# Values loaded at level 8, pooling sums as scans, the gate ahead of the root, heads 2 and 3 between more products, and the last tile's end in two pieces

## The chip, the cores and the metric

The kernel runs on one core of a Trainium2 chip. The core has a matrix engine (TensorE, PE in the profile), three engines for element work (VectorE or DVE, ScalarE or ACT, GpSimd or POOL) and a queue of transfers that SyncE (SP) issues in program order. The metric is the device time of one execution in microseconds (us); lower is better.

## The reference

A decoder layer is computed for 1024 tokens of width 1024, with 16 learned tokens ahead. Two mixers run in parallel on the normed input. One is a gated linear recurrence of four heads of 128, the other takes moving averages over 2, 4, 8 and 16 tokens. Each goes through its branch matrix and a sigmoid gate. The sum goes through an output matrix and a norm into the residual, and a gated feed-forward part with a short convolution follows. Cut to what matters here:

```python
def hgrn2(q, f_logit, i, g, lb, out_gain):
    f = lb + (1.0 - lb) * jax.nn.sigmoid(fl)
    k = (1.0 - lb) * jax.nn.sigmoid(-fl)
    ...   # state = exp(b_last) * state + k_dec^T v ;  o = q*exp(b) @ state + scores @ v, in chunks of 64
    o = o * lax.rsqrt(jnp.mean(o * o, axis=-1, keepdims=True) + EPS)
    o = o.reshape(bsz, L, HGRN_WIDTH) * out_gain
    return o * jax.nn.sigmoid(g)

def multiscale_pool(v, proj, scale):
    ...   # per group of 128 columns and window w in (2, 4, 8, 16):
        outs.append((hi - lo) / cnt - vg[:, :, gi])       # mean of the last w tokens, minus the token
    y = jnp.einsum('blgc,gcd->blgd', pooled, proj)

def reference(...):
        u = rmsnorm(h, mix_norm_pre[l])
        q, f_logit, i_in, g_out, v_pool, gate_a, gate_b = jnp.split(u @ w_in[l], cuts, axis=-1)
        a = hgrn2(q, f_logit, i_in, g_out, lbs[l], hgrn_out_norm[l])
        p = multiscale_pool(v_pool, pool_proj[l], pool_scale[l])
        z = sigmoid(gate_a) * (a @ w_branch_hgrn[l]) + sigmoid(gate_b) * (p @ w_branch_pool[l])
        h = h + rmsnorm(z @ w_out[l], mix_norm_post[l])
        u = rmsnorm(h, ffn_norm_pre[l])
        gt = causal_dwconv(u @ ffn_w_gate[l], ffn_conv_w[l], ffn_conv_b[l])
        y = (jax.nn.gelu(gt) * (u @ ffn_w_up[l])) @ ffn_w_down[l]
        h = h + rmsnorm(y, ffn_norm_post[l])
```

## The kernel before

Every matrix product is made of three products of split operands (hi by hi, hi by lo, lo by hi), so each weight block is loaded (`wraw`), rounded on ScalarE (`whi`) and its rest taken on VectorE (`wlo`). The large products use Strassen's scheme. In time the kernel has these stages:

1. 0–110 us: the values of the heads (`pv`), written to DRAM (`vscr`; the 16 learned tokens' in `vmscr`).
2. 110–325 us: the gates' and the heads' inputs by Strassen (`P`). Each head's f, q, k and kb (k over f) are stored in DRAM (`fscr`, `qscr`, `kscr`, `kbscr`), and so is its output gate (`gscr`).
3. 325–525 us: the heads, the pooling projections (`ppv` for the values, `ppp` for the outputs), two more output gates (`pg`) and the branch products (`pbb` for pooling, then `pba` for the heads).
4. 525–700 us: the output matrix (`pm`). To 1110 us the feed-forward's first matrices, to 1287 us its second by Strassen (`pd`), then the last half and the end of each 128-token tile.

The change is in stage 3 and in the end of stage 4. In stage 3 a head is a generator, `head_steps`: load f, q, kb and k; products within blocks of 2 (`sb`); then for each level 2, 4, ..., 64 the products of neighbouring blocks (`sl`, from `level_mm`), the decays multiplied into k and q (`grow`, VectorE) and the scores copied out (`level_out`); then k transposed (`pt`, `kt`), the chunks' state sums (`ds`, `st`), the output (`po`, `o`), and its mean square by products with ones (`ms`), the root by Ln and Exp on ScalarE, and the norm. All loads of a head go through SyncE's queue. The head's values (`vh`) are loaded behind its last level.

The string `ORDER` writes out what is issued in turn: h0 to h3 is a head's next step, `PVa1`/`PVb1` half of a pooling value product, `sp` the pooling split of a group, `G` an output gate product, `PP` a pooling projection, `sa` the split of a head's output for the branch products, `BB` and `BA` the branch products, `w0`–`w5` the rounding and storing in DRAM (`kept0h` and so on) of feed-forward weights for later. A scheduler of the framework then orders each engine's instructions by their dependences and this program order; in blocks named `manual_schedule` the written order holds. Tiles come from pools: 26 slots for tiles of a row's length, three buffers for each of `wraw`, `whi` and `wlo`, eight banks for products. A load of the heads or of a gate is issued behind the latest weight load in SyncE's queue (`tc.issue_after`).

Pooling: `post_pv` makes the sum of the last w values of group g by log2(w) passes of VectorE, each adding the sum shifted by 1, 2, 4, 8 (L817). `pool_split` sets the 15th column of the window 16 from a reduction (L827), divides, subtracts the value and splits (`plh`, `pll`).

The end: after the last shared products of stage 4 each of the four tiles in `c11` gets its last 18 half products, a subtraction (L1743), a square with its sum (L1667), the gain (L1668), the root and the addition to the residual (L1680, `finish`).

Of the kernel before, what the change touches and what calls it, by code (L numbers as in the profile page):

```python
# [12 lines left out]
ALU = mybir.AluOpType  # L13
# [39 lines left out]
ZA = 4  # L53
AHEAD = 3

ORDER = ("h0 h1 PV0 PVa1 h0 h1 PVb1 h0 h1 h0 PVa2 h1 sp0 h0 h1 PVb2 h0 h1 sp1 h0 h1 h2 PVa3 h0 h1 sp2 h0 h3 "
         "PVb3 h1 h0 h1 h0 h1 h2 Ga2 sp3 h0 h1 h2 h3 Gb2 h2 h3 sa0 PP0 PP1 h2 h3 Ga3 h2 h3 h2 Gb3 h3 h2 h3 PP2 PP3 h2 h3 sa1 h2 h3 w0 w1 "
         "BB0 w4 h2 h3 w4 BB1 h2 h3 BB2 sa2 h3 BB3 w5 BB4 sa3 w4 w5 BB5 w5 BB6 BB7 w5 BA0 w2 BA1 w3 BA2 BA4 BA3 BA5 BA6 BA7")
POOLED = ()
TRUNC = False  # L60

CH_ALL = [(0, 348), (348, 346), (694, 346)]
# [4 lines left out]
def trunk_kernel(ctx: ExitStack, tc: tile.TileContext, x, meta_tokens, mix_norm_pre,  # L67
# [29 lines left out]
    def slot(n, dtype=F32, name="s"):  # L97
        return stage["fm", "p"].tile([P, n], dtype, tag="fm", name=nm(name), padded_shape=[P, LP])
# [4 lines left out]
    def bank(name="ps"):  # L103
        return stage["ps", "p"].tile([P, 512], F32, tag="ps", name=nm(name))
# [11 lines left out]
    def small(shape, name, tag, bufs=4):  # L116
        return sm.tile(shape, F32, tag=tag, name=nm(name), bufs=bufs)
# [63 lines left out]
    def mm3(ps, a, b, first, last):  # L181
        (ahi, alo), (bhi, blo) = a, b
        pe.matmul(ps, ahi, bhi, start=first, stop=False)  # L183
        pe.matmul(ps, ahi, blo, start=False, stop=False)  # L184
        pe.matmul(ps, alo, bhi, start=False, stop=last)  # L185
# [421 lines left out]
    def eng(op):  # L607
        return pool_e if op in POOLED else dve

# [40 lines left out]
    def head_steps(h):  # L650
# [68 lines left out]
                            ps[:, : NCH * SB].rearrange("p (c t) -> p c t", c=NCH))  # L719
        yield  # L720
        for lv in LEVELS:
            if lv == NM:
                pm = bank("sm")
                for i in range(HALO):
                    pe.matmul(pm[:NM, i : i + 1], k[:, i * NM : (i + 1) * NM], q[:, NM + T0 + i : NM + T0 + i + 1],
                              start=True, stop=True)
                act.copy(scm, pm[:NM, :HALO])
# [10 lines left out]
        with tc.issue_after(stage["load"].ins):  # L738
            nc.sync.dma_start(vmeta, vmd[:, h * P : (h + 1) * P])
            nc.sync.dma_start(heads[h]["v"].rearrange("p (c v) -> p c v", c=NCH),  # L740
                              vd[:, :, h * P : (h + 1) * P].rearrange("c p v -> p c v"))
        kt = slot(NCH * P, name="kt")
        for j in range(2):
            pt = bank("pt")
# [42 lines left out]
            act.copy(o[:, HALO + j * 512 : HALO + (j + 1) * 512], ps)  # L787
        act.activation(rs, o, AF.Square)
        rh, rl = split(rs, "r", eng(f"rsl.{h}"))
        yield  # L790
        for lo, n in CH_Q:
            ps = bank("ms")
# [1 line left out]
            pe.matmul(ps[:, :n], onesr, rl[:, lo : lo + n], start=False, stop=True)  # L794
            act.activation(rs[:, lo : lo + n], ps[:, :n], AF.Ln, bias=eps_t)
        act.activation(rs, rs, AF.Exp, scale=-0.5)
        dve.scalar_tensor_tensor(o, o, ong[:, h : h + 1], rs, ALU.mult, ALU.mult)
        eng(f"osg.{h}").tensor_tensor(o, o, sgs[h], ALU.mult)
        heads[h] = dict(o=o)


# [2 lines left out]

    def post_pv(g, pv):
        w = POOL_WINDOWS[g]
        vp, s1 = slot(L, name="vp"), slot(L, name="s1")
        s2 = slot(L, name="s2") if w > 2 else None
        for (lo, n), ps in zip(CH_ALL, pv):
            act.copy(vp[:, lo : lo + n], ps[:, :n])  # L810
        cur, step = vp, 1
        bufs = [s1, s2]
        while step < w:
            nxt = bufs[0]
            bufs = bufs[::-1]
            a = 2 * step - 1
            dve.tensor_tensor(nxt[:, a:L], cur[:, a:L], cur[:, a - step : L - step], ALU.add)  # L817
            cur, step = nxt, 2 * step
        pooled[g] = (cur, vp)

    def pool_split(g):
        w = POOL_WINDOWS[g]
        cur, vp = pooled[g]
        if w > T0 + 1:

            c1 = small([P, 1], "c1", "c1", 2)
            dve.tensor_reduce(c1, vp[:, 0 : T0 + 1], mybir.AxisListType.X, ALU.add)  # L827
            dve.tensor_scalar(cur[:, T0 : T0 + 1], c1, float(w) / (T0 + 1), None, ALU.mult)
        dve.scalar_tensor_tensor(cur[:, T0:L], cur[:, T0:L], 1.0 / w, vp[:, T0:L], ALU.mult, ALU.subtract)
        pin[g] = split(cur[:, T0:L], "pl")  # L830

    def split(src, name, eng=dve):
        hi, lo_ = slot(TQ, F32R, name + "h"), slot(TQ, F32R, name + "l")
        act.copy(hi, src)
        eng.tensor_tensor(lo_, src, rr(hi), ALU.subtract)
        return hi, lo_
# [828 lines left out]
    def half_norm(src, t, j):  # L1665

        act.activation(junk, src, AF.Square, accum_out=ssq4[:, j, t : t + 1])  # L1667
# [55 lines left out]


    banks = [bank("pd") for _ in range(NT)]
    for n, k in enumerate(range(KT, KH)):
        if n == 0:
            prep_last(KH - 2, False)
            for t in range(NT):
                dve.tensor_tensor(c12[t], c12[t], pb[t], ALU.add)  # L1730
            prep_last(KH - 1, False)
        multiply(banks, held.pop(k), n == 0, False)
        if n < NT:
            half_norm(c22[n], NT + n, 1)
            half_norm(c21[n], NT + n, 0)
            finish(NT + n, c21[n], c22[n])
            load_h(n)
        if n > 0:
            half_norm(c12[n - 1], n - 1, 1)
    for t in range(NT):  # L1740
        for j in range(KT):
            multiply(banks, held[j], False, j == KT - 1, [t])
        dve.tensor_tensor(c11[t], banks[t], c11[t], ALU.subtract)  # L1743
        half_norm(c11[t], t, 0)
        finish(t, c11[t], c12[t])
    close_pool("ps", "sm", "fm")


# [27 lines left out]
```

## Time and profile before

| | us |
|---|---|
| median of 3 runs (lowest, highest) | 1327.94 (1326.75, 1328.4) |
| the profiled execution | 1327.77 |
| its span | 1326.0 |
| TensorE busy | 1292.2 (97%) |
| VectorE busy | 964.4 (73%) |
| ScalarE busy | 524.2 (40%) |
| GpSimd busy | 356.7 (27%) |

The span runs from the first to the last instruction that the profile has; 1.77 us lie around it. A row of the timeline gives start, duration, engine, line, operation, tiles, shape, and in brackets the idle time ahead of it with what ended it. A row of the stretches gives the stretch, its length, the busy time and count of TensorE, of its weight loads, of VectorE, ScalarE and GpSimd, the clock that TensorE was granted (1.00 is full), the busy share of the DMA engines, and GB/s.

### The profile page before, as it was taken

Reading aid. Unit: us, or ns where it says so; the run is one execution under the profiler, and the core shown is the slowest. Engines: PE = TensorE matmul, PEld = TensorE weight load, DVE = VectorE, ACT = ScalarE, POOL = GpSimd, SP = SyncE. Lnnn points to the kernel's source line nnn. Section 1 sums busy time; section 2 is a strip of 40 time slices with the busy share of each in tenths; the row PEclk is TensorE's granted clock in tenths of the full one; section 3 lists DMA queues with packets and bytes.
Section 4 is the critical chain, followed back from the end, with each engine's and each line's share of the span. In section 5 each row is a group of like instructions: output and inputs, shape, how many; then the busy total and the mean of one; then the engine's idle time right before and its main releaser. Section 6 shows DMA issues by size and latency. Waiting matters only on the chain.

```text
span 1326.0 us, 21946 instructions
## 1 busy us (share of the span) xinstructions
PE 1292.2 (97%) x8617; PEld 1144.3 (86%) x8617; DVE 964.4 (73%) x1297; ACT 524.2 (40%) x903; POOL 356.7 (27%) x303
## 2 busy tenths in 40 slices
PE   8999999999988889999999999999999999999997
PEld 7799899999988789987898888888888888888886
DVE  6768965444677866775578999888998885455757
ACT  5554533333137444235564322222222233444443
POOL 3015333220000000061025555545555652000000
PEclk9999999999989989999999999999999999999999
DMA  7135643334341276887686677677767799666644
GB/s 273 42 106 175 198 147 104 112 109 144 121 151 49 79 248 230 311 279 258 229 286 234 180 208 191 191 207 176 174 157 165 162 250 304 216 223 222 222 174 159
DMA packets 143802, 247.62 MB, mean 187 GB/s; under 512 B 11000, under 2 KB 75164, under 8 KB 143698
## 3 DMA queue, kind: packets, MB, share of 16 engines
q1 hardware_dynamic: 131634, 221.83, 49.4%
q0 software_dynamic: 12064, 24.38, 11.0%
q8 instruction: 68, 1.11, 0.3%
q14 instruction: 36, 0.29, 0.1%
HBM read 174.11 MB, written 95.09 MB: 203 GB/s over the span
## 4 chain that ended last, share of the span: by engine, by line
PE 94%; issue 2%; ACT 2%; DMA 1%; DVE 1%; SPq 0%; DVEq 0%; ACTq 0%
PE P L303 17%; PE P L304 17%; PE P L306 17%; PE pd L183 5%; PE pd L184 5%; PE pd L185 5%; PE pm L183 2%; PE pm L184 2%; PE pm L185 2%; PE pbb L203 1%; PE pbb L204 1%; PE pbb L207 1%; PE pba L203 1%; PE pv L184 1%; PE pba L204 1%
## 5 line engine op out<-in xcount | busy, mean ns | idle before, releaser
L304 PE MATMUL P<-v,whi 128*128 128x512 f32 (+2 forms) x408 | 140.7, 353 | 0.0
L303 PE MATMUL P<-v,whi 128*128 128x512 f32 (+2 forms) x408 | 140.7, 352 | 0.0
L306 PE MATMUL P<-v,wlo 128*128 128x512 f32 (+2 forms) x424 | 135.1, 349 | 0.0
L274 POOL TENSOR_TENSOR swa<-wraw,wraw 128x512 f32<-128x512 f32 x32 | 51.0, 1595 | 190.7 <-DMA wraw<-in_w_in_dram 77.5
L248 ACT CAST whi<-wraw 128x512 fp32r<-128x512 f32 x90 | 53.1, 618 | 102.2 <-PE P L304 75.7
L1510 DVE TENSOR_TENSOR rot<-wraw,rot 128x1024 fp32r<-128x1024 f32 x31 | 38.0, 1224 | 72.3 <-ACT rot L1509 72.2
L303 PEld LDWEIGHTS P<-v,whi 128*128 128x128 f32 x408 | 76.7, 188 | 10.4
L304 PEld LDWEIGHTS P<-v,whi 128*128 128x128 f32 x408 | 76.6, 188 | 10.2
L306 PEld LDWEIGHTS P<-v,wlo 128*128 128x128 f32 x424 | 74.1, 188 | 10.8
L184 PE MATMUL pd<-rot 128*128 128x512 f32 x272 | 82.1, 389 | 0.0
L185 PE MATMUL pd<-rot 128*128 128x512 f32 x272 | 82.1, 389 | 0.0
L183 PE MATMUL pd<-rot 128*128 128x512 f32 x272 | 81.1, 389 | 0.1
L249 DVE TENSOR_TENSOR wlo<-wraw,whi 128x512 fp32r<-128x512 f32 x86 | 73.3, 875 | 2.7 <-ACT whi L248 2.7
L248 ACT CAST whi<-swa 128x512 fp32r<-128x512 f32 x64 | 38.1, 618 | 92.2 <-PE P L304 77.2
L249 DVE TENSOR_TENSOR wlo<-swb,whi 128x512 fp32r<-128x512 f32 x64 | 66.1, 1040 | 9.8 <-ACT whi L248 9.8
L1509 ACT CAST rot<-wraw 128x1024 fp32r<-128x1024 f32 x31 | 32.7, 1054 | 90.7 <-PE pd L185 89.4
L303 PE MATMUL P<-uhi,whi 128*128 128x258 f32 (+2 forms) x240 | 68.5, 303 | 0.0
L304 PE MATMUL P<-ulo,whi 128*128 128x258 f32 (+2 forms) x240 | 68.4, 303 | 0.0
L248 ACT CAST whi<-swb 128x512 fp32r<-128x512 f32 x64 | 38.2, 618 | 71.9 <-PE P L304 67.4
L303 PE MATMUL P<-t4h,whi 128*128 128x258 f32 (+2 forms) x228 | 65.5, 304 | 0.0
L303 PE MATMUL P<-t2h,whi 128*128 128x258 f32 (+2 forms) x228 | 65.3, 304 | 0.1
L304 PE MATMUL P<-t4l,whi 128*128 128x258 f32 (+2 forms) x228 | 65.3, 304 | 0.0
(380 smaller groups left out, 3841.1 us busy)
## 6 DMA issues: line engine op xcount, KB each, us to landing
wraw<-in_w_in_dram SPq DMA_DIRECT2D x36, 512.0 KB, 4.5
yt<-ysum SPq DMA_DIRECT2D x33, 512.0 KB, 5.5
wraw<-in_ffn_w_gate_dram SPq DMA_DIRECT2D x26, 512.0 KB, 5.8
wraw<-in_ffn_w_up_dram SPq DMA_DIRECT2D x22, 512.0 KB, 5.7
wsum<-in_ffn_w_down_dram SPq DMA_DIRECT2D x22, 512.0 KB, 8.4
wraw<-in_w_out_dram SPq DMA_DIRECT2D x18, 512.0 KB, 5.3
ysum<-ys SPq DMA_DIRECT2D x11, 768.0 KB, 6.1
sa<-sscr SPq DMA_DIRECT2D x16, 513.0 KB, 5.7
```

What stands on the lines that cost most here:

```text
L183: pe.matmul(ps, ahi, bhi, start=first, stop=False)
L184: pe.matmul(ps, ahi, blo, start=False, stop=False)
L185: pe.matmul(ps, alo, bhi, start=False, stop=last)
L203: pe.matmul(ps[:, :n], whi[:, k, :], xhi, start=(k == 0), stop=False)
L248: act.copy(hi, src)
L249: (pool_e if 4 <= i < 2 * self.early else dve).tensor_tensor(lo, src, rr(hi), ALU.subtract)
L274: pool_e.tensor_tensor(s1, a21, a22, ALU.add)
L303: pe.matmul(d, whi[:, k, :], xh[:, c : c + w], start=(k == 0 and onto is None), stop=False, **go)
L304: pe.matmul(d, whi[:, k, :], xl[:, c : c + w], start=False, stop=False, **go)
L306: pe.matmul(x[:, o : o + w], wlo[:, k, :], xh[:, c : c + w], start=False, stop=(k == 3), **go)
L1509: act.copy(hi, src)
L1510: dve.tensor_tensor(lo, src, rr(hi), ALU.subtract)
```

## The change

It has five parts.

- The values of a head are loaded ahead of its level 8 (`VLOAD`) and not behind its last level.
- The sum over the last w values is a scan of VectorE (add the new value, subtract the one w back) for w = 4, 8 and 16. The values' tile gets 16 cleared columns ahead. The window 2 stays one addition, and the reduction for the 15th column goes, since the scan holds that sum.
- The multiplication of a head's output by its gain and its gate stands ahead of the root products. After the root only the product with the root remains, where both were before.
- `ORDER` changes: head 2's and 3's first steps come later, and their levels stand between more products (the third gate, the pooling projections, the branch products BB0 to BB5); the kept weights' steps and the splits of heads 2 and 3 move with them.
- At the end the last tile's sums are made in two pieces of 256 columns in two banks, so that the first piece's subtraction, square and gain run during the second's products; ScalarE and VectorE keep the written order there, and the gain's product goes to a tile of its own, `left`. The first tile's `c12` sum moves ahead of the last prepared weights.

The diff, cut to its core:

```diff
+ORDER = ("h0 h1 PV0 PVa1 h0 h1 PVb1 h0 h1 h0 PVa2 h1 sp0 h0 h1 PVb2 h0 h1 sp1 h0 h1 h2 PVa3 h0 h1 sp2 h0 "
+         "PVb3 h1 h0 h1 h0 h1 Ga2 sp3 h0 h1 h2 h3 Gb2 h2 h3 sa0 Ga3 h2 h3 PP0 PP1 Gb3 h2 h3 sa1 PP2 PP3 h2 h3 w0 w1 "
+         "BB0 w4 h2 h3 h2 w4 BB1 h3 h2 h3 BB2 h2 h3 BB3 h2 w5 h3 BB4 h2 h3 w4 sa2 w5 BB5 h3 w5 sa3 BB6 BB7 w5 BA0 w2 BA1 w3 BA2 "
...
+VLOAD = 8
...
         for lv in LEVELS:
+            if lv == VLOAD:
+                heads[h]["v"] = slot(NCH * P, name="vh")
+                vmeta = small([NM, P], "vmeta", "vmeta", 2)
+                with tc.issue_after(stage["load"].ins):
+                    nc.sync.dma_start(vmeta, vmd[:, h * P : (h + 1) * P])
+                    nc.sync.dma_start(heads[h]["v"].rearrange("p (c v) -> p c v", c=NCH),
+                                      vd[:, :, h * P : (h + 1) * P].rearrange("c p v -> p c v"))
...
-        heads[h]["v"] = slot(NCH * P, name="vh")
-        vmeta = small([NM, P], "vmeta", "vmeta", 2)
...
         rh, rl = split(rs, "r", eng(f"rsl.{h}"))
+        dve.scalar_tensor_tensor(o, o, ong[:, h : h + 1], sgs[h], ALU.mult, ALU.mult)
         yield
...
-        dve.scalar_tensor_tensor(o, o, ong[:, h : h + 1], rs, ALU.mult, ALU.mult)
-        eng(f"osg.{h}").tensor_tensor(o, o, sgs[h], ALU.mult)
+        dve.tensor_tensor(o, o, rs, ALU.mult)
...
-        vp, s1 = slot(L, name="vp"), slot(L, name="s1")
-        s2 = slot(L, name="s2") if w > 2 else None
+        vz, cur = slot(NM + L, name="vp"), slot(L, name="s1")
+        vp = vz[:, NM:]
+        pool_e.memset(vz[:, :NM], 0.0)
...
-        while step < w:
...
-            dve.tensor_tensor(nxt[:, a:L], cur[:, a:L], cur[:, a - step : L - step], ALU.add)
+        if w == 2:
+            dve.tensor_tensor(cur, vp, vz[:, NM - 1 : NM - 1 + L], ALU.add)
+        else:
+            dve.tensor_tensor_scan(cur, vp, vz[:, NM - w : NM - w + L], 0.0, ALU.add, ALU.subtract)
...
-            dve.tensor_reduce(c1, vp[:, 0 : T0 + 1], mybir.AxisListType.X, ALU.add)
-            dve.tensor_scalar(cur[:, T0 : T0 + 1], c1, float(w) / (T0 + 1), None, ALU.mult)
+            dve.tensor_scalar(cur[:, T0 : T0 + 1], cur[:, T0 : T0 + 1], float(w) / (T0 + 1), None, ALU.mult)
...
+    pieces = [(banks[-1], slice(0, 256)), (bank("pd"), slice(256, 512))]
...
+            dve.tensor_tensor(c12[0], c12[0], pb[0], ALU.add)
             prep_last(KH - 2, False)
-            for t in range(NT):
+            for t in range(1, NT):
                 dve.tensor_tensor(c12[t], c12[t], pb[t], ALU.add)
             prep_last(KH - 1, False)
-        multiply(banks, held.pop(k), n == 0, False)
+        ops = held.pop(k)
+        multiply(banks, ops, n == 0, False, range(NT - 1))
+        multiply_pieces(ops, n == 0, False)
...
+    lefts = [slot(512, name="left") for _ in range(2)]
+    sums4 = small([P, 1], "sums4", "mq", 6)
+    with tc.manual_schedule(engines={E.Activation, E.DVE}):
+        for t in range(NT):
+            left = lefts[t % 2]
+            for i, (ps, n) in enumerate(pieces if t == NT - 1 else ((banks[t], slice(0, 512)),)):
+                for j in range(KT):
+                    if t == NT - 1:
+                        multiply_pieces(held[j], False, j == KT - 1, pieces[i : i + 1])
+                    else:
+                        multiply(banks, held[j], False, j == KT - 1, [t])
+                dve.tensor_tensor(c11[t][:, n], ps[:, : n.stop - n.start], c11[t][:, n], ALU.subtract)
+                part = t == NT - 1 and i == 0
+                act.activation(junk[:, n], c11[t][:, n], AF.Square, accum_out=sums4 if part else ssq4[:, 0, t : t + 1])
+                dve.tensor_tensor(left[:, n], c11[t][:, n], g4[:, n], ALU.mult)
+                if part:
+                    dve.scalar_tensor_tensor(ssq4[:, 1, t : t + 1], sums4, 1.0 / D, ssq4[:, 1, t : t + 1],
+                                             ALU.mult, ALU.add)
+            finish(t, left, c12[t])
```

More of the change, by code (lines that the diff above doesn't have):

```diff
@@ L54 @@
 AHEAD = 3
-ORDER = ("h0 h1 PV0 PVa1 h0 h1 PVb1 h0 h1 h0 PVa2 h1 sp0 h0 h1 PVb2 h0 h1 sp1 h0 h1 h2 PVa3 h0 h1 sp2 h0 h3 "
-         "PVb3 h1 h0 h1 h0 h1 h2 Ga2 sp3 h0 h1 h2 h3 Gb2 h2 h3 sa0 PP0 PP1 h2 h3 Ga3 h2 h3 h2 Gb3 h3 h2 h3 PP2 PP3 h2 h3 sa1 h2 h3 w0 w1 "
-         "BB0 w4 h2 h3 w4 BB1 h2 h3 BB2 sa2 h3 BB3 w5 BB4 sa3 w4 w5 BB5 w5 BB6 BB7 w5 BA0 w2 BA1 w3 BA2 BA4 BA3 BA5 BA6 BA7")
+ORDER = ("h0 h1 PV0 PVa1 h0 h1 PVb1 h0 h1 h0 PVa2 h1 sp0 h0 h1 PVb2 h0 h1 sp1 h0 h1 h2 PVa3 h0 h1 sp2 h0 "
+         "PVb3 h1 h0 h1 h0 h1 Ga2 sp3 h0 h1 h2 h3 Gb2 h2 h3 sa0 Ga3 h2 h3 PP0 PP1 Gb3 h2 h3 sa1 PP2 PP3 h2 h3 w0 w1 "
+         "BB0 w4 h2 h3 h2 w4 BB1 h3 h2 h3 BB2 h2 h3 BB3 h2 w5 h3 BB4 h2 h3 w4 sa2 w5 BB5 h3 w5 sa3 BB6 BB7 w5 BA0 w2 BA1 w3 BA2 "
+         "BA4 BA3 BA5 BA6 BA7")
 POOLED = ()
+VLOAD = 8
 TRUNC = False
@@ L734, in head_steps @@
             yield
-        heads[h]["v"] = slot(NCH * P, name="vh")
-        vmeta = small([NM, P], "vmeta", "vmeta", 2)
[L738 to L741, printed above, removed]
         kt = slot(NCH * P, name="kt")
@@ L824, in pool_split @@
         if w > T0 + 1:
-            c1 = small([P, 1], "c1", "c1", 2)
-            dve.tensor_reduce(c1, vp[:, 0 : T0 + 1], mybir.AxisListType.X, ALU.add)
-            dve.tensor_scalar(cur[:, T0 : T0 + 1], c1, float(w) / (T0 + 1), None, ALU.mult)
+            dve.tensor_scalar(cur[:, T0 : T0 + 1], cur[:, T0 : T0 + 1], float(w) / (T0 + 1), None, ALU.mult)
         dve.scalar_tensor_tensor(cur[:, T0:L], cur[:, T0:L], 1.0 / w, vp[:, T0:L], ALU.mult, ALU.subtract)
@@ L1725, in trunk_kernel, with multiply_pieces @@
     banks = [bank("pd") for _ in range(NT)]
+    pieces = [(banks[-1], slice(0, 256)), (bank("pd"), slice(256, 512))]
+    def multiply_pieces(ops, first, last, which=pieces):
+        (yh, yl), (wh, wl) = ops
+        tt = slice((NT - 1) * P, NT * P)
+        for ps, n in which:
+            mm3(ps[:, :256], (yh[:, tt], yl[:, tt]), (wh[:, n], wl[:, n]), first, last)
     for n, k in enumerate(range(KT, KH)):
         if n == 0:
+            dve.tensor_tensor(c12[0], c12[0], pb[0], ALU.add)
             prep_last(KH - 2, False)
-            for t in range(NT):
+            for t in range(1, NT):
                 dve.tensor_tensor(c12[t], c12[t], pb[t], ALU.add)
             prep_last(KH - 1, False)
-        multiply(banks, held.pop(k), n == 0, False)
+        ops = held.pop(k)
+        multiply(banks, ops, n == 0, False, range(NT - 1))
+        multiply_pieces(ops, n == 0, False)
         if n < NT:
@@ L1739, in trunk_kernel @@
             half_norm(c12[n - 1], n - 1, 1)
[L1740 to L1745, printed above, removed]
+    lefts = [slot(512, name="left") for _ in range(2)]
[17 more added lines that the diff above has]
+            finish(t, left, c12[t])
     close_pool("ps", "sm", "fm")
```

6 lines of the change are left out of this document (removed).

## The prediction

> **What bounds the kernel now.** I read first the chain that ended last, then TensorE's share by stage, then what ended its idle times. The chain is TensorE's own work nearly everywhere, so only time in which TensorE stands idle or runs at a lower clock can be won, apart from the very end.
>
> ```profile
> PE 94%; issue 2%; ACT 2%; DMA 1%; DVE 1%; SPq 0%; DVEq 0%; ACTq 0%
> ```
>
> The stretches (span, TensorE busy with its count, the other engines, granted clock, DMA share) show where that time lies: in the stage of the recurrence heads.
>
> ```profile
> 350.00:400.00 50.00, 42.51 (x804) 40.19 (x802) 38.25 (x65) 16.22 (x37) 0.95 (x6) 0.90 0.36 121
> 400.00:450.00 50.00, 44.06 (x853) 42.28 (x853) 37.55 (x69) 27.26 (x44) 1.91 (x2) 0.97 0.18 55
> 450.00:500.00 50.00, 41.88 (x385) 39.97 (x380) 34.24 (x64) 29.51 (x55) 0.00 (x0) 0.90 0.62 200
> ```
>
> Idle are 50.00 − 42.51 = 7.5, 5.9 and 8.1 us, together 21.5. VectorE, the third pair, is busy for three quarters of the time, and the releasers of TensorE's waits name it in turn with the loads of the heads' values:
>
> ```profile
> PE ds L764 <- DMA vh<-vscr: 6.9, 2, 5.2
> PE sl L687 <- DVE q L676: 3.5, 2, 2.1
> ```
>
> One by one (start, duration, line, shape, idle before it and its releaser):
>
> ```profile
> 374.69 0.70 PE L687 MATMUL sl<-q,k 128*32 128x32 f32 x32 [2.10 <-DVE q L676]
> 377.24 1.07 PE L687 MATMUL sl<-q,k 128*32 128x32 f32 x32 [1.85 <-ACT sc L702]
> 400.41 1.80 PE L764 MATMUL ds<-vh,kt 128*128 128x128 f32 x14 [1.69 <-DMA vh<-vscr]
> 428.69 0.73 PE L693 MATMUL sl<-q,k 128*32 128x16 f32 x64 [2.13 <-issue]
> 433.97 0.75 PE L693 MATMUL sl<-q,k 128*32 128x16 f32 x64 [1.53 <-DVE near L708]
> 436.59 0.73 PE L693 MATMUL sl<-q,k 128*32 128x16 f32 x64 [1.87 <-DVE q L676]
> 455.92 0.70 PE L687 MATMUL sl<-q,k 128*32 128x32 f32 x32 [1.44 <-DVE q L676]
> 463.46 0.48 PE L757 MATMUL ds<-vmeta,ktm 16*128 16x128 f32 x2 [0.52 <-ACT ktm L752]
> 469.12 3.33 PE L764 MATMUL ds<-vh,kt 128*128 128x128 f32 x14 [5.17 <-DMA vh<-vscr]
> ```
>
> Beside the idle time stands the granted clock (the last column but two), which falls around these gaps:
>
> ```profile
> 355.00:360.00 5.00, 4.77 (x44) 4.63 (x33) 5.00 (x8) 0.00 (x0) 0.00 (x0) 0.66 0.29 84
> 435.00:440.00 5.00, 3.41 (x74) 3.42 (x75) 5.00 (x13) 0.00 (x0) 0.00 (x0) 0.74 0.47 137
> 465.00:470.00 5.00, 0.89 (x4) 0.92 (x5) 3.50 (x6) 2.09 (x5) 0.00 (x0) 0.50 1.04 340
> 470.00:475.00 5.00, 5.00 (x25) 4.92 (x25) 2.43 (x7) 1.31 (x3) 0.00 (x0) 0.51 0.97 316
> ```
>
> At a clock of 0.51 the 5.00 us of work of 470–475 would have taken 2.55, and the 0.89 at 0.50 half of that: 0.89×0.50 + 5.00×0.49 = 2.9 us lost. In 435–440 it is 3.41×0.26 = 0.9.
>
> **The values' loads.** The waits at 400.41 and 469.12 follow loads that SyncE's queue issued late:
>
> ```profile
> 396.20 0.37 SPq L740 DMA_DIRECT2D vh<-vscr  x1
> 462.41 0.48 SPq L740 DMA_DIRECT2D vh<-vscr  x1
> ```
>
> From the second to its use are 469.12 − 462.41 = 6.7 us. SyncE's queue in the order of the program, before, from head 2's inputs on:
>
> ```order
> L146 DMA wraw_4757<-in_pool_proj_dram 128x128
> L653 DMA f_4133<-fscr 128x1056
> L654 DMA q_4136<-qscr 128x1026
> L655 DMA kb_4135<-kbscr 128x1024
> L656 DMA k_4134<-kscr 128x1056
> L740 DMA vh_4211<-vscr 128x8x128
> L653 DMA f_4232<-fscr 128x1056
> L654 DMA q_4235<-qscr 128x1026
> L655 DMA kb_4234<-kbscr 128x1024
> L656 DMA k_4233<-kscr 128x1056
> L146 DMA wraw_4783<-in_pool_proj_dram 128x128
> L740 DMA vh_4292<-vscr 128x8x128
> ```
>
> and in the changed kernel, where both values of heads 0 and 1 (vh_3869, vh_3910) stand first and head 3's inputs (f_4524 and on) come after the gates:
>
> ```order
> L148 DMA wraw_4568<-in_pool_proj_dram 128x128
> L729 DMA vh_3869<-vscr 128x8x128
> L729 DMA vh_3910<-vscr 128x8x128
> L148 DMA wraw_4789<-in_pool_proj_dram 128x128
> L655 DMA f_4139<-fscr 128x1056
> L656 DMA q_4142<-qscr 128x1026
> L657 DMA kb_4141<-kbscr 128x1024
> L658 DMA k_4140<-kscr 128x1056
> L148 DMA wraw_4795<-in_pool_proj_dram 128x128
> L778 DMA sg_4342<-gscr 128x1026
> L778 DMA sg_4375<-gscr 128x1026
> L655 DMA f_4524<-fscr 128x1056
> ```
>
> Heads 0 and 1 then have their values before head 2's inputs are even asked for, and the DMA engines have room (share 0.29 in 355–360). Those of heads 2 and 3 are now issued at level 8, ahead of the kept weights' stores that stood before them. Taken: −1.7 at 400.41 and −5.2 at 469.12, and the clock of 465–475, −2.9. What is late next at 400.41 is ScalarE's kt copy, hidden by head 0's own products (nothing to nothing; if the cover fails, up to 1.7 comes back).
>
> Head 3's inputs are issued later by the two gates' loads, which wait for head 1's state. Their landing takes
>
> ```profile
> k<-kscr SPq DMA_DIRECT2D x4, 528.0 KB, 8.1
> ```
>
> and between head 1's root and head 3's first level stand 19 + 36 branch products (at the 0.159 us worked out below, 8.7) and head 2's first two levels. I take 0.3, between 0 and 3.
>
> **Scans and VectorE's order.** Ten pooling passes become one pass and three scans, and the reduction goes. A pass costs
>
> ```profile
> L817 DVE TENSOR_TENSOR s<-vp 128x1039 f32<-128x1039 f32 x4 | 5.0, 1246 | 0.6 <-ACT scm L727 0.6
> ```
>
> No scan is in the trace. One pass, 1.25, bounds it below; a running sum that adds and subtracts is two such passes, 2.5, which I take; three passes, 3.7, bound it above. VectorE is relieved by 10×1.25 − 1.25 − 3×2.5 = 3.75 us (7.5 with one pass, nothing with three). [...] Only the place matters, 374–377: before, two short passes lie around the two heads' k and q; now one scan lies between them, and head 0's k and q come ahead of it. Head 0 so gains at most the one pass that stood before it, less a wider low-part pass (128x1024 for 128x128, about 0.9) that now does: 0.4 at 374.69. Head 1 has one scan of 2.5 where one pass of 1.25 was, so it loses 2.5 − 1.25 − 0.4 = 0.8 at 377.24. Together +0.4 (−0.8 to +2).
>
> **Heads 2 and 3 over more products.** Their levels now stand singly between gate, pooling and branch products, so the 428–437 gaps, 2.13 + 1.53 + 1.87 = 5.5, shrink where a product lies between a level's multiply and its use. Three remain by the order: head 3's level 2, whose load is last (0.2), head 2's level 16 behind head 3's masks (1.6), head 3's level 8 behind a pooling low part (1.2): 3.0. These are estimates from the VectorE passes (0.7 to 1.25 each) that stand between. So −2.5 (−1 to −4), and the clock of 435–440, −0.8.
>
> What else is idle in 450–500, 8.12 − 5.17 = 2.95, is replaced by other gaps. VectorE now has the first kept sums and low parts ahead of the levels 32 of heads 2 and 3, at
>
> ```profile
> L920 DVE TENSOR_TENSOR wlo<-wraw,wraw 128x512 f32<-128x512 f32 x2 | 1.3, 690 | 1.6 <-DMA wraw<-in_ffn_w_gate_dram 1.6
> 504.48 1.35 DVE L879 TENSOR_TENSOR sa<-sa,pbb 128x342 f32<-128x342 f32 x3
> ```
>
> Head 2's level 64 waits for one to six of the 0.69 us passes (0.6 to 4), head 3's for up to four of them and a 1.35 group (0 to 4.8), and the transposes 0 to 1. I take 6.0 of 0.6 to 9.8, the upper half, since these passes themselves wait for weights loaded behind the stores: +3.0. Such gaps also lower the clock: 355–360 stood at 0.66 after gaps of about 2 us, 4.77×0.34 = 1.6 lost. I take +1.5 (0 to 2.9). [...]
>
> **Head 3's end.** TensorE's place: the last root products of head 3 (ms) and the first branch product that needs its output (pba); before 163 branch products lie between, now
>
> ```order
> L798 MATMUL ms_5727<-rl_5649,onesr 128x342
> L798 MATMUL ms_5731<-rl_5649,onesr 128x342
> L798 MATMUL ms_5735<-rl_5649,onesr 128x342
> L205 MATMUL pbb_5759<-phi_4801,whi_5490 128x342
> ...
> L209 MATMUL pbb_5807<-phi_4997,wlo_5491 128x342
> L205 MATMUL pba_5860<-ah_4660,whi_5712 128x342
> L206 MATMUL pba_5860<-al_4661,whi_5712 128x342
> ```
>
> 48, and 18 of the first output products before the fourth head's turn. VectorE there, after (al_5752 is head 3's low part, wlo_5846 the next weights'):
>
> ```order
> L920 TENSOR_TENSOR wlo_5742<-wlo_5742,whi_5741 128x512
> L801 TENSOR_TENSOR o_5622<-o_5622,rs_5623 128x1026
> L162 TENSOR_TENSOR wlo_5846<-wraw_5844,whi_5845 128x1024
> L832 TENSOR_TENSOR al_5752<-o_5622,ah_5751 128x1026
> ```
>
> so al now stands behind a pass whose buffer a store (kept8l) must leave. Before:
>
> ```profile
> 506.07 0.65 PE L794 MATMUL ms<-rl,onesr 128*128 128x342 f32 x3
> 510.27 1.29 DVE L797 SCALAR_TENSOR_TENSOR o<-o,par,rs 128x1026 f32<-128x1026 f32 x1 [1.63 <-ACT rs L796]
> 514.50 0.32 PE L203 MATMUL pbb<-phi,whi 128*128 128x342 f32 x1
> 514.84 1.23 DVE L835 TENSOR_TENSOR al<-o,ah 128x1026 fp32r<-128x1026 f32 x1 [0.52 <-ACT ah L834]
> 519.12 0.63 PE L207 MATMUL pbb<-phi,wlo 128*128 128x342 f32 x3
> 525.59 0.55 SPq L937 DMA_DIRECT2D kept7l<-wlo  x1
> 530.81 0.69 DVE L920 TENSOR_TENSOR wlo<-wraw,wraw 128x512 f32<-128x512 f32 x1 [2.61 <-DMA kept7l<-wlo]
> ```
>
> The 29 matmuls from 514.50 to 519.12 give 0.159 each, so 66 cover 10.5 us. The chain from the end of the root products (506.72) to al's end (516.07) is 9.4, less the multiply moved ahead of the root (1.2): 8.2. With a store of 530.81 − 525.59 = 5.2 that starts 2 to 4 after the root and 1.2 for each of the two passes, al ends 9.6 to 11.6 after it. So 0 to 1.1 is lost, and 3 if the store starts 2 later still. Taken: +0.5.
>
> **The tail.** The last tile's 33 products of 512 become 66 of 256. Rows of both widths:
>
> ```profile
> 1316.80 0.39 PE L183 MATMUL pd<-yh 128*128 128x512 f32 x1
> ...
> 1318.61 0.39 PE L185 MATMUL pd<-yh,yl 128*128 128x512 f32 x1
> 1319.04 0.69 DVE L1743 TENSOR_TENSOR acc<-pd,acc 128x512 f32<-128x512 f32 x1 [0.39 <-PE pd L185]
> 1319.76 0.63 ACT L1667 ACTIVATE junk<-acc 128x512 f32<-128x512 f32 x1 [3.03 <-DVE acc L1743]
> 1321.32 1.42 DVE L1680 SCALAR_TENSOR_TENSOR hrow<-acc,rstd,hrow 128x512 f32<-128x512 f32 x2
> ...
> 875.53 0.28 PE L303 MATMUL P<-v,whi 128*128 128x258 f32 x1
> 876.96 0.28 PE L303 MATMUL P<-v,whi 128*128 128x258 f32 x1
> ```
>
> From 1316.80 to 1318.61 are eight matmuls, 0.226 each; from 875.53 to 876.96 twelve of 256 and 258, 0.119 each. The split costs 33×(2×0.119 − 0.226) = 0.4. Halving the subtraction and the square (0.69 and 0.63) takes about 0.6 off the end: −0.2 (−0.6 to +0.3). The rest of the chain to the output is the same. Clearing the pooling margin on GpSimd, the early loads of the meta values and the early sum of c12 cost nothing: the first two have idle engines, the third is hidden by TensorE's product on the other banks (0.7 if that cover is gone).
>
> **Sum.** −1.7 − 5.2 − 2.9 + 0.3 + 0.4 − 2.5 − 0.8 + 3.0 + 1.5 + 0.5 − 0.2 = −7.6. The profiled execution took 1327.77 (span 1326.0 and 1.77 around it), 0.17 under the median of the three shown, 1327.94: I predict 1320.2.
>
> **Rivals.** (A) The stall only moves: the level-64 waits reach 9.8 instead of 6.0 and bring the whole 2.9 of clock back (+3.8 + 1.4), so 1325.4; 428–437 not shrinking (+2.5) makes 1327.9. For it speaks that VectorE is at 5.00 of 5.00 in 435–440; against it, that its queue gets shorter. (B) The slow side: VectorE works in order, and the kept weights' passes that now stand in the heads' chains (before the levels 32 and before head 3's al) wait for stores out of their buffers, as the pass at 530.81 did for 5.2 us. Each such wait passes whole to a level or to the first pba once it is over its cover (none at level 64, 10.5 − 8.2 = 2.3 at pba). Two of 5.2 beyond what is taken make 1320.2 + 10.4 = 1330.6; from 7.6 on the gain is gone. For it speaks that VectorE waited 2.61 for a store at that row; against it, that the values' loads now go ahead of the stores. (C) The scan costs three passes and head 1 waits for all of it: +1.6, 1321.8, still faster. [...]
>
> **Chances.** Forecast 0.40, C 0.15, D 0.13, all faster; A 0.17, of it 0.13 within ±0.2% (2.7 us, about what a measurement of this kernel can tell from no change) and 0.04 above; B 0.15, of it 0.02 within and 0.13 above. So faster 0.68, same 0.15, slower 0.17. With all terms at their low ends (−1.7 − 5.2 − 2.9 − 0.8 − 4 − 0.8 − 2.4 − 0.6 = −18.4) it would be 1309.4, which is unlikely at once; the range goes from 1313 to 1330, where it leaves out half of B.
>
> **What would show it.** Right: no TensorE wait ended by a load of vh; clock about 1.00 where 465–475 was; TensorE idle in 350–500 near 14 instead of 21.5; one wait of 1 to 4 us before level 64 of heads 2 and 3, ended by q or k of VectorE; a scan row near 2.5 us; no idle TensorE at the first pba; the last subtraction 256 wide. Wrong: a wait over 3 us at pba ended by al, a scan of several us with TensorE waiting behind it, or waits for head 3's k.

## The result, and the profile after

The changed kernel takes 1329.01 us in the median of 20 runs (1327.6 to 1331.57), the kernel before 1327.12 of 20 (1324.01 to 1331.19). The ratio is 1.0017, 95% interval 1.0010 to 1.0024: slower by about 2 us, where 7.6 us less were forecast. The profiled execution of the changed kernel took 1327.76, near its fastest run (1.25 under its median), and that of before 1327.77, above 16 of its 20 runs (0.65 over its median). So the two traces are equally long: they show where the forecast gain went, and only the medians show the further 1.9 us.

TensorE's waits in the head stage and the branch products (320 to 600 us), after:

```profile
PE sl L689 <- DVE q L678: 9.2, 4, 2.9
PE pt L753 <- DVE sa L876: 3.5, 1, 3.5
PE po L780 <- ACT rs L799: 2.3, 1, 2.3
PE sl L695 <- DVE q L678: 2.0, 1, 2.0
PE sl L695 <- DVE near L710: 1.6, 1, 1.6
PE sl L695 <- DVE plo L839: 0.9, 1, 0.9
```

The columns are the wait's total, its count and the longest. No wait is ended by a load of vh any more: that part did what it says. Two waits are new, at head 3's transposes (pt) and at its output (po). The stretches, in the columns of before, and two of 5 us behind the new waits:

```profile
350.00:400.00 50.00, 43.28 (x813) 41.06 (x812) 36.85 (x60) 17.12 (x39) 0.87 (x5) 0.90 0.25 80
400.00:450.00 50.00, 47.48 (x851) 45.59 (x851) 37.55 (x67) 32.33 (x52) 2.05 (x4) 0.98 0.42 131
450.00:500.00 50.00, 41.95 (x396) 39.66 (x396) 31.27 (x63) 18.86 (x38) 0.00 (x0) 0.92 0.59 195
500.00:550.00 50.00, 47.27 (x295) 46.37 (x294) 36.08 (x58) 24.99 (x37) 0.00 (x0) 0.97 0.71 237
485.00:490.00 5.00, 4.40 (x19) 4.11 (x20) 3.78 (x10) 1.38 (x4) 0.00 (x0) 0.66 0.00 2
510.00:515.00 5.00, 5.00 (x33) 5.00 (x32) 4.18 (x7) 3.44 (x4) 0.00 (x0) 0.75 0.32 120
```

400–450 gained 3.4 us of TensorE's time. 450–500 stayed where it was, and 500–550, which had no idle TensorE before, now has 2.7. In 350–500 TensorE is idle for 17.3 us, where the prediction had about 14 of the former 21.5. One number sums this up, and the experiments use it: the **head loss**, which is the idle time of TensorE plus its busy time at the missing share of the clock, in stretches of 5 us from 325 to 540. That a lower clock stretches the work shows in the trace of before: 14 products of ds of one shape took 1.80 us at 1.00 (400.41) and 3.33 at 0.50 (469.12). The head loss was 22.4 + 8.5 = 30.9 us before, and is 20.9 + 9.7 = 30.6 after.

The first new wait, along its chain (SyncE, VectorE, TensorE):

```profile
475.28 3.69 SPq L946 DMA_DIRECT2D wraw<-in_ffn_w_up_dram  x2
481.26 0.34 SPq L872 DMA_DIRECT2D sa<-sscr  x1
484.99 1.35 DVE L876 TENSOR_TENSOR sa<-sa,pbb 128x342 f32<-128x342 f32 x3 [6.43 <-DMA sa<-sscr]
485.56 0.38 PE L753 MATMUL pt<-ident,k 128*16 128x128 f32 x1 [3.50 <-DVE sa L876]
486.35 2.65 DVE L770 SCALAR_TENSOR_TENSOR st<-st,f,ds 128x128 f32<-128x128 f32 x7
```

A branch product must be multiplied by its gate, `sa`, before its bank is free. The gate's load is issued at 481.26, at the end of head 2's state products (ds), and SyncE's waits give the reason:

```profile
SPq L872 <- PE ds L767: 2.2, 1, 2.2
```

The load needs one of the 26 row slots, and ds gave the last one back. VectorE multiplied the gate in only at 484.99. By then it had stood 6.43 us idle with head 2's states (st) behind it in its order, TensorE 3.50 at the transposes for want of a bank, and the clock of 485–490 was 0.66.

The second new wait (VectorE, ScalarE, TensorE):

```profile
504.30 1.29 DVE L917 TENSOR_TENSOR wlo<-wraw,wraw 128x512 f32<-128x512 f32 x2 [0.37 <-DMA kept7l<-wlo]
505.63 0.62 ACT L919 CAST whi<-wlo 128x512 fp32r<-128x512 f32 x1 [4.77 <-DVE wlo L917]
506.26 1.28 ACT L799 ACT_TABLE_LOAD   x1
507.56 1.42 ACT L799 ACTIVATE rs<-ms,eps_t 128x342 f32<-128x342 f32 x3
508.16 0.38 PE L780 MATMUL po<-scm,vmeta 16*128 16x2 f32 x2 [2.26 <-ACT rs L799]
```

A kept weight's cast (L919) stands ahead of head 2's Ln (L799) on ScalarE and waits 4.77 us for VectorE's pass (L917), which waited for the store kept7l, issued at 499.49. The cast itself held the root only briefly: it ended at 506.25, the last of the root's products (ms) at 505.90. But the table load of 1.28 us that goes ahead of Ln also stood behind the cast, and so came after the products too. Only Ln frees the banks of the root's products, and head 3's output needs a bank.

### The profile page after: what moved, and what is told of

Its sections match the earlier page's. It is cut to its first block, busy times and chain, and to the rows that moved or that the text cites. A ratio compares the mean times of both kernels' runs of the same rounds, so it can differ in the third digit from the quotient of the medians.

```text
span 1326.1 us, 22015 instructions
## 1 busy us (share of the span) xinstructions
PE 1294.3 (98%) x8650; PEld 1146.5 (86%) x8650; DVE 962.7 (73%) x1293; ACT 524.8 (40%) x905; POOL 357.6 (27%) x307
## 4 chain that ended last, share of the span: by engine, by line
PE 67%; DVE 2%; issue 2%; DMA 1%; ACT 1%; SPq 0%; DVEq 0%; ACTq 0%
PE P L306 11%; PE P L305 11%; PE P L308 11%; PE pd L185 5%; PE pd L187 5%; PE pd L186 5%; PE pm L185 2%; PE pm L186 2%; PE pm L187 2%; PE pba L205 1%; PE pba L206 1%; PE pba L209 1%; PE pbb L205 1%; PE pbb L206 1%; PE pbb L209 1%
## 5 line engine op out<-in xcount | busy, mean ns | idle before, releaser
L251 DVE TENSOR_TENSOR wlo<-wraw,whi 128x512 fp32r<-128x512 f32 x86 | 76.2, 909 | 2.7 <-ACT whi L250 2.7
L251 DVE TENSOR_TENSOR wlo<-swb,whi 128x512 fp32r<-128x512 f32 x64 | 69.0, 1086 | 9.7 <-ACT whi L250 9.7
```

The costliest lines, as they stand in the source:

```text
L251: (pool_e if 4 <= i < 2 * self.early else dve).tensor_tensor(lo, src, rr(hi), ALU.subtract)
```

## The experiments

Every kernel was timed in five rounds (5 to 12 runs) beside runs of before on the same chip. Ratios are to before; "the changed kernel" is 1.0017 (1.0010 to 1.0024).

**The old order.** `ORDER` as before, the other four parts as changed:

```diff
...
-         "BB0 w4 h2 h3 h2 w4 BB1 h3 h2 h3 BB2 h2 h3 BB3 h2 w5 h3 BB4 h2 h3 w4 sa2 w5 BB5 h3 w5 sa3 BB6 BB7 w5 BA0 ...
+         "BB0 w4 h2 h3 w4 BB1 h2 h3 BB2 sa2 h3 BB3 w5 BB4 sa3 w4 w5 BB5 w5 BB6 BB7 w5 BA0 ...
```

> The changed kernel with the order string of before; the other four parts stay. Theory 1 (the new order costs what the other parts bring: the transposes of head 3 waiting 3.5 us for a gate load, its output waiting 2.3 us behind the second head's root on ScalarE, each with 1.3 to 1.5 us of lower clock): with the old order these two waits are gone, the waits for the values' loads stay away, and the time is 5 to 9 us under the changed kernel, 1320 to 1324. Theory 2 (values loaded early take slots and queue places that something else needs in either order, so a wait of the same size appears elsewhere): 1327 to 1330, with a new wait of 3 to 6 us in 440 to 520.

Measured: 1323.63 us, 0.9975 (0.9965 to 0.9985), head loss 26.0. The wait at the transposes is gone. At the output 1.33 us are left, behind the same Ln:

```profile
486.05 1.28 ACT L798 ACT_TABLE_LOAD   x1 [0.71 <-PE ms L797]
487.95 0.38 PE L779 MATMUL po<-scm,vmeta 16*128 16x2 f32 x2 [1.33 <-ACT rs L798]
```

Theory 1 holds in its time: on top of the other four parts the new order costs 0.42%, 5.6 us, and turns a gain into a loss. That both waits would go was too much: wherever the old order has early values, head 3's output waits for this root, 1.33 to 3.01 us in five kernels, so the new order alone is not its cause.

**The old tail.** The last tile in one piece again:

```diff
...
-        multiply(banks, ops, n == 0, False, range(NT - 1))
-        multiply_pieces(ops, n == 0, False)
+        multiply(banks, held.pop(k), n == 0, False)
...
```

> The changed kernel with the last tile's end in one piece, as before. Theory 1 (the tail is worth what the prediction said, 0.2 us): 1329 to 1329.5, no difference that can be told. Theory 2 (the 0.4 us of more products and the order written out by hand cost more than the pieces bring, and the tail is a good part of the 1.9 us lost): 1327.5 to 1328.2.

Measured: 1330.54, 1.0023 (1.0014 to 1.0031), above both theories. The interval overlaps the changed kernel's, so the tail is not what lost the time.

**A slot more.** The changed kernel with

```diff
-FM_SLOTS = 26
-LP = 1088
+FM_SLOTS = 27
+LP = 1056
```

> The changed kernel with 27 slots for rows in place of 26; the room comes from shorter padding of the rows (1056 for 1088). No operation is added or left out. Theory 1 (the gate load at 481.26 was late because its slot was freed only by head 2's state products, after which the branch products' banks and with them head 3's transposes waited 3.5 us, with 1.5 of clock): the gate is loaded before 475, the transposes do not wait, and the time is 3 to 5 us lower, 1324 to 1326. Theory 2 (the gate load was late because SyncE's queue stood behind the kept weights' loads and stores; a slot more changes nothing): the same wait at the transposes, 1328.5 to 1329.5.

Measured: 1325.08, 0.9984 (0.9976 to 0.9993). The wait at the transposes is gone. VectorE there, in this kernel, whose stage began 3.1 us later:

```profile
481.04 1.23 DVE L162 TENSOR_TENSOR wlo<-wraw,whi 128x1024 fp32r<-128x1024 f32 x1 [2.25 <-DMA kept6l<-wlo]
482.25 1.35 DVE L876 TENSOR_TENSOR sa<-sa,pbb 128x342 f32<-128x342 f32 x3
485.04 2.65 DVE L770 SCALAR_TENSOR_TENSOR st<-st,f,ds 128x128 f32<-128x128 f32 x7 [1.43 <-ACT st L761]
```

The first gate no longer waits for its load, which is now issued at 471.76. Without the 27th slot it also stood further back in SyncE's queue, behind the two kept-weight loads of 475.28. Of the two theories the slot's holds, and the control below sizes it. Head 3's output still waits, 1.54 us behind head 2's root.

**Kept weights late.** The changed kernel with

```diff
-... BB3 h2 w5 h3 BB4 h2 h3 w4 sa2 w5 BB5 h3 w5 sa3 BB6 BB7 w5 BA0 ...
+... BB3 h2 h3 BB4 h2 h3 sa2 BB5 h3 sa3 w5 BB6 w4 BB7 w5 w5 w5 BA0 ...
```

> The changed kernel with its last five kept-weight steps moved in the order string from between BB3 and BB7 to behind the split of head 3's output. Theory 1 (the output products of head 3 waited 2.3 us because ScalarE's cast of a kept weight, itself waiting for a store, stood ahead of head 2's root): that wait goes, and also the weight loads ahead of the gate load, so 3 to 8 us less, 1321 to 1326. Theory 2 (the order of ScalarE's work is not what held the root, but the table load and VectorE): the wait stays within 0.5 us of 2.3 and the time is 1328 to 1330; or the kept weights now come late for the first output products (a wait of some us at pba), 1329 to 1333.

Measured: 1327.51, 1.0001 (0.9992 to 1.0009), 1.5 us under the changed kernel. Head 3's output does not wait any more, and there is no wait at pba (1.3 us are new at the output matrix, pm). Without the cast ahead of it, the table load is done long before the root's products end, and Ln follows them at once:

```profile
502.73 1.28 ACT L799 ACT_TABLE_LOAD   x1
507.48 1.42 ACT L799 ACTIVATE rs<-ms,eps_t 128x342 f32<-128x342 f32 x3 [3.46 <-PE ms L798]
```

The wait at the transposes is still there (3.92), although one of the two kept-weight loads now stands behind the gate's:

```profile
485.68 1.35 DVE L876 TENSOR_TENSOR sa<-sa,pbb 128x342 f32<-128x342 f32 x3 [6.52 <-DMA sa<-sscr]
```

Theory 1 was right for the output and wrong for the gate load, which hangs on the slot.

**The control for the slot.** Short rows and 26 slots:

```diff
-LP = 1088
+LP = 1056
```

> The changed kernel with rows padded to 1056 and still 26 slots: the control for the 27th slot. Theory 1 (the slot alone made the 27-slot kernel faster, and the padding is neutral): 1328 to 1330, with the 3.5 us wait of head 3's transposes in place. Theory 2 (the padding costs: in the 27-slot kernel the pooling products began 3.1 us later, at 329.84 against 326.73): 1331 to 1332.5, so that the slot alone is worth 6 to 7. Theory 3 (the padding made the gain): 1324.5 to 1326, with the wait still there or not.

Measured: 1333.21, 1.0054 (1.0042 to 1.0067), head loss 34.5, with both waits:

```profile
PE pt L753 <- DVE sa L876: 4.3, 1, 4.3
PE po L780 <- ACT rs L799: 2.5, 1, 2.5
```

Even theory 2 had it too low. Short rows cost 0.37% by themselves, and the 27th slot alone, in this layout, is worth 1.0054 − 0.9984 = 0.70%, 9.3 us (0.5 to 0.9% by the two intervals); the head loss is 8.5 lower with it (26.0).

**Both.** 27 slots with short rows, and the kept weights late:

> The changed kernel with 27 slots (rows padded to 1056) and the last five kept-weight steps late. Theory 1 (two separate waits, one for a slot and one behind a kept weight on ScalarE, carry the loss of the new order): both waits gone and 1320.5 to 1323.5, as the two gains of 3.9 and 1.5 add up. Theory 2 (what one wait gives back the next takes): 1324.5 to 1326, with another wait of 2 us or more in 480 to 530.

Measured: 1322.5, 0.9967 (0.9955 to 0.9978), head loss 20.8, the lowest of all. From 440 us on TensorE has left:

```profile
PE sl L689 <- DVE q L678: 5.6, 2, 3.8
PE sl L695 <- DVE near L710: 1.6, 1, 1.6
PE sl L695 <- DVE plo L839: 0.8, 1, 0.8
PE pm L185 <- DVE sa L876: 0.5, 1, 0.5
```

Neither wait came back in 480 to 530, where theory 2 had put one. Head 2's level 64, at 463, waits longer here: 3.78 us, against 2.15 in the changed kernel. Against the control with the same short rows, the two repairs together took 10.7 us off. This is the new order as it was meant, 4.9 us under before in spite of the short rows; it is not shown to be faster than the old order with early values (0.9975).

**Where the short rows cost.** The same with the two large operands at a pitch of 1072, and only the slots at 1056:

```diff
-LP = 1056
+LP = 1072
...
-... name=nm(name), padded_shape=[P, LP])       # slot
+... name=nm(name), padded_shape=[P, NM + L])
```

> The changed kernel with 27 slots and the last five kept-weight steps late, where the rows in slots are padded to 1056 but the two large operands keep a pitch of 1072 in place of 1056. Theory 1 (the pitch of the large operands is what cost 3.6 us before 330 us and about 5 in all in the short-row control): 1317.5 to 1320. Theory 2 (the padding of the slots cost it): 1322 to 1323, as with the pitch of 1056.

Measured: 1322.86, 0.9973 (0.9962 to 0.9983), no gain, and theory 2's time. The pooling products began at 328.42, against 330.30 with 1056 and 326.73 with 1088 for both, so the pitch shifts the early stage, but the total does not follow: this trace's head loss is 24.4 against 20.8, all of it clock (9.6 against 4.9; the idle time is lower, 14.8 against 15.9). What the short rows cost beyond the early stage, and where, stays open.

**Without scans, old order.** Early values, early gate and tail, and the shifted additions again:

```diff
...
-            dve.tensor_tensor_scan(cur, vp, vz[:, NM - w : NM - w + L], 0.0, ALU.add, ALU.subtract)
...
+            dve.tensor_tensor(nxt[:, a:L], cur[:, a:L], cur[:, a - step : L - step], ALU.add)
...
```

> The changed kernel with the order string of before and the pooling sums as shifted additions again; early values, early gate and the tail stay. Theory 1 (a scan of 2.31 us is short enough for its places, and its relief of VectorE helps): slower than the old order with scans, whose median was 1323.6, by 1 to 2 us. Theory 2 (where a scan stands between the two heads' level multiplies, at 371 to 383, it holds one level 1 us longer than a single pass did: 5.84 us of idle TensorE there with scans against 3.95 before, and more low clock): 1 to 3 us faster, 1321 to 1322.5.

Measured: 1321.97, 0.9963 (0.9950 to 0.9976), head loss 24.7; this and the kernel with both repairs are the fastest. The intervals with and without scans overlap (0.9975 and 0.9963), so the times do not tell them apart; the traces show what the scan does at its place. First the old order with scans, then without, VectorE's scan and TensorE's two waits:

```profile
372.31 2.32 DVE L817 TENSOR_TENSOR_SCAN s<-vp 128x1040 f32<-128x1040 f32 x1 [0.66 <-ACT scm L735]
375.96 1.07 PE L688 MATMUL sl<-q,k 128*32 128x32 f32 x32 [3.23 <-DVE q L677]
379.64 1.07 PE L688 MATMUL sl<-q,k 128*32 128x32 f32 x32 [2.61 <-ACT plh L830]
```

```profile
374.28 0.70 PE L688 MATMUL sl<-q,k 128*32 128x32 f32 x32 [2.10 <-DVE q L677]
376.83 1.07 PE L688 MATMUL sl<-q,k 128*32 128x32 f32 x32 [1.85 <-ACT sc L703]
```

The scan takes the place of a 1.24 us pass ahead of head 0's k and q, and the two waits grow by 1.9 us.

**Without early values, old order.**

```diff
-            if lv == VLOAD:
-                heads[h]["v"] = slot(NCH * P, name="vh")
...
+        heads[h]["v"] = slot(NCH * P, name="vh")       # behind the last level
```

> The changed kernel with the order string of before and the values loaded behind the last level again; scans, early gate and the tail stay. Theory 1 (the values' loads carry the gain of the old order): the waits of 1.7 and 5.2 us for the values return with the 2.5 to 2.9 of clock behind the second, so 1323.6 + 7 to 9 = 1331, slower than before by what the scans cost. Theory 2 (the gain comes from scans, gate and tail, and the values' wait would be hidden by what else is late): 1323 to 1326.

Measured: 1328.04, 1.0008 (1.0000 to 1.0017), head loss 30.9. That is between the theories: in the old order the early values are worth 0.33%, 4.4 us. The waits of 1.3 and 4.7 us for them are back:

```profile
467.93 3.32 PE L765 MATMUL ds<-vh,kt 128*128 128x128 f32 x14 [4.74 <-DMA vh<-vscr]
```

**Early values alone**, on the kernel before:

> The kernel before with the values loaded ahead of level 8, and nothing else. Theory 1 (this part alone carries the gain): 1319 to 1323, with the 6.9 us of waits for values gone and the clock near 470 back. Theory 2 (the earlier loads only uncover the next wait, on slots or VectorE): 1325 to 1328, a new wait of 3 us or more in 455 to 480.

Measured: 1324.46, 0.9986 (0.9973 to 0.9999), between the theories, with runs from 1322.08 to 1330.57. In its profile the waits for values are gone, and head 3's output has a new one of 1.63.

**The old order and 27 slots**, with short rows:

> The changed kernel with the order string of before and 27 slots (rows padded to 1056). Theory 1 (the slot is short only where heads 2 and 3 lie between the branch products, so with the old order a 27th slot has little to free): 1322.5 to 1324, as without it. Theory 2 (a slot is short in both orders): 2 to 4 us less, 1319.5 to 1321.5.

Measured: 1326.41, 0.9996 (0.9985 to 1.0006), slower than with 26: neither theory, as both left out the rows' cost. And the same order without scans, with the pitch of 1072:

> The order of before with early values, early gate and the tail, without scans, and with 27 slots in the layout of 1072 and 1056. Theory 1 (in the old order the slot is not short, as the 27-slot run of that order did not gain even against a cost of padding of 5): 1321 to 1323, as with 26 slots. Theory 2 (there too a slot was short, hidden by the padding's cost): 1317 to 1319.

Measured: 1324.88, 0.9982 (0.9974 to 0.9991); 1321.97 without the slot. Neither theory's range holds it; in the old order the slot does not pay for the layout.

**The tail alone** and **the gate alone**, each on the kernel before (the tail as in the change; the gate's edit is shown):

```diff
+        dve.scalar_tensor_tensor(o, o, ong[:, h : h + 1], sgs[h], ALU.mult, ALU.mult)
...
-        dve.scalar_tensor_tensor(o, o, ong[:, h : h + 1], rs, ALU.mult, ALU.mult)
-        eng(f"osg.{h}").tensor_tensor(o, o, sgs[h], ALU.mult)
+        dve.tensor_tensor(o, o, rs, ALU.mult)
```

> The kernel before with the last tile's end in two pieces and nothing else. Theory 1 (prediction, 0.2 us): 1326.5 to 1327.3. Theory 2 (worth more, as taking it out of the changed kernel made that 1.5 us slower in its median): 1325.3 to 1326.2.

> The kernel before with the gate's multiplication ahead of the root, and nothing else. Theory 1 (the chain it shortens lies under 26 us of branch products for head 3 and under gate products for the others, so it is hidden): 1326.5 to 1327.5. Theory 2 (early values, gate and tail together gave 4.9 us and early values alone 2.4, so the gate is worth 1 to 2): 1325 to 1326.

Measured: 1327.16, 1.0001 (0.9992 to 1.0010), and 1328.20, 1.0011 (0.9998 to 1.0023), neither told from no change; the gate's median lies above both theories. The tail-only kernel also says how far one profile can be trusted: its heads are those of before, and its head loss was 27.7 against 30.9.

**The new order alone**, on the kernel before:

> The kernel before with the new order string and nothing else. Theory 1 (the new order is slower by itself, through the slot and the kept weights between the heads' steps; the early values only add to the lack of slots): 1329 to 1333, with the values' wait of several us there as well as waits in 480 to 515. Theory 2 (the new order is bad only together with early values, which hold a slot longer): 1324 to 1328, no wait over 2 us at head 3's transposes.

Measured: 1327.13, 1.0009 (1.0000 to 1.0019): theory 2's time. By itself the new order costs 0.2% at most, on top of the other four parts 0.42%. Head 3's transposes do not wait in it; the waits are at the root's products (3.47 and 3.22, behind ScalarE).

**The new order with both repairs and without scans**, with the pitch of 1072:

> The changed kernel with late kept weights and 27 slots in the layout of 1072 and 1056, and without scans. Theory 1 (scans cost 1 to 2 us in either order, at 371 to 383): 1 to 2 us under the same kernel with scans. Theory 2 (in the new order the scans' relief of VectorE pays for them): the same within 0.7 us, or slower.

Measured: 1330.21, 1.0025 (1.0012 to 1.0039), 0.5% above the same with scans: theory 1 falls. Theory 2 allowed for slower, but its reason has nothing of 7 us in it. The head losses (25.3 against 24.4) do not carry that; the two profiled executions lie only 2.6 apart. Why scans pay there and seem to cost in the old order is not settled.

## Why the prediction was wrong

The forecast was faster by 7.6 us; the measured time lies in the range, but on the other side of no change. Step by step:

- **Values (−9.8).** The mechanism was right: no wait for vh is left. The size was not: alone −0.14%, in the old order −0.33%, 2 to 4 us. In the old order, with early values against without, TensorE's idle time in the heads fell by 5.7 us (23.6 to 17.9), but what the clock lost did not fall (7.2 to 8.2): it was lost behind other gaps, 3.2 us in 430–440 against 1.6. The term took the whole wait and its whole clock as won; of the two, the wait came nearly whole.
- **Scans (+0.4).** A scan took 2.31 us, between the 1.25 of one pass and the 3.7 of three, by the row

```profile
L818 DVE TENSOR_TENSOR_SCAN s<-vp 128x1040 f32<-128x1040 f32 x3 | 6.9, 2311 | 0.6 <-ACT vp L814 0.6
```

  so the two passes that were taken were right. A scan is 1.9 times the plain pass of that width in the same trace (L816, 128x1040, 1.24). The cost at 374–377 came near to what was worked out: head 0 gained 0.3 (1.78), head 1 lost 1.1 (2.92), so +0.75 for +0.4.
- **Heads 2 and 3 over more products (−2.5, −0.8, +3.0, +1.5).** The shrinking of 428–437 was right: 5.5 became 2.5 at 445–450, though its clock stayed (1.3 lost before, 1.2 after). The level-64 waits (2.15 and 2.37, taken 6.0 in all with the transposes) were right or high. **This is the step that failed: it priced the transposes at 0 to 1 us and the output not at all.** They cost 3.50 and 2.26, with 1.5 us of clock behind each. So level 64, transposes and output came to 10.3 us of idle time and 4.5 of clock (1.54 in 470–475, 1.50 in 485–490, 1.48 in 505–515), where 6.0 and 1.5 were taken. These 7.3 us are nearly the whole 7.6 by which the two traces miss the forecast; the other terms' errors nearly cancel. The further 1.9 us between the medians are not in these traces.

  The reason was left out in both waits. A transpose needs a bank, a bank needs its gate's load, and that load needs a row slot. Early values hold one more of them: here head 3's were asked for at 444.79, ahead of that gate's load at 481.26. The new order without early values asks for them behind the last level, and its transposes did not wait. And Ln with its table load stands behind casts of kept weights on ScalarE. The two waits taken away one by one and together (0.9984, 1.0001, 0.9967) show that they carry the loss.
- **Head 3's end (+0.5).** Right in that it did not decide: VectorE's al ended at 532.7, with no idle TensorE at the first pba, which followed at 532.79.
- **The tail (−0.2).** Not refuted: alone 1.0001, which cannot tell 0.2 us from none. From the start of the last subtraction to the addition to the residual it is 1.52 us now and was 2.28, so the end is 0.76 shorter, where 0.6 was taken; what the split of the products cost the two traces do not separate.
- **Rivals.** (A), the stall only moves, came nearest: 1325.4 to 1327.9 for 1329. Its place was wrong. (B) had the right kind, an engine in order held by a transfer (VectorE 6.43 us, by the load of sa), and named kept weights; of its two places, the levels 32 and al, neither was the one. (C) was wrong in its cost: a scan took 2.31, under two passes, and head 1 lost 1.1 by it. As for the clock, gaps of 2.02 us at 354 and 2.26 at 508 have low clock behind them (0.66 in 355–360, 0.91 and 0.75 in 505–515), and in another kernel a gap of 2.02 us had 1.00 behind it, as the last section shows: so the clock terms (−2.9, −0.8, +1.5), each read off one trace, could be off by such a gap's 1.7 us either way.

## What to carry to other kernels

Before an early load is counted as won, count what it holds: a slot, a bank, a place in a queue, and who asks for one next. When steps of one chain are spread between other work, look through the order of every engine that they cross, and at what stands there ahead of each step and waits for a transfer: here a cast of a weight for much later waited 4.77 us on ScalarE and pushed the table load of a root behind the products that it should have met, and TensorE stood 2.26 us. A rearrangement and the resource it needs are one change; tried without the slot, the new order looked bad, and with it and late kept weights it was 4.9 us under the kernel before.

## What the runs showed of the hardware

The rows' padding, with no change in the work, cost 0.37% (1056 against 1088 columns), part of it ahead of the heads. All 18 traces agree there: the pooling products began at 325.8 to 327.6 us with 1088, at 328.4 with 1072 and at 329.4 to 330.3 with 1056. Of the 240 matmuls P<-uhi,whi of that stage the median is 282 ns and the longest 389 in the changed kernel, 283 and 473 with the short rows and 26 slots, 283 and 397 with the short rows, 27 slots and late kept weights. Why is open.

The granted clock behind the same gap differs from kernel to kernel where TensorE's instructions are the same. The tail-only kernel and the one with early values alone both have a gap of 2.02 us at 354 and the same pooling products behind it:

```profile
355.00:360.00 5.00, 5.00 (x33) 4.97 (x31) 5.00 (x9) 0.00 (x0) 0.00 (x0) 0.66 0.23 68
355.00:360.00 5.00, 5.00 (x33) 5.00 (x33) 5.00 (x10) 0.00 (x0) 0.00 (x0) 1.00 0.93 245
```

The first lost 1.7 us to the clock, the second nothing. So one trace does not give the price of such a gap.
